# Two-layer retention and convolution backbone on one core: output and down projections by seven products, with the token sums made a stage earlier

## The chip, the cores and the metric

The kernel runs on one core of a Trainium2 chip. The metric is device time in microseconds (us) of one execution; for the kernel before, three runs gave 2707.88, 2707.94 and 2709.12, median 2707.94. Engines are called PE (TensorE, matrix products), DVE (VectorE), ACT (ScalarE), POOL (GpSimd) and SP (SyncE, which here only issues DMAs). PSUM, where PE accumulates, has eight banks of 128 x 512 fp32.

## What is computed

Two layers over 1024 latent tokens of width 1024, with a 256-token context that layer 0 reads. Layer 0 mixes tokens by retention (4 heads), layer 1 by a gated short convolution; each is followed by a SwiGLU FFN of hidden width 2816. Every sub-layer is modulated and gated by parameters made from `c`.

```python
def retention_output(o, g, w_o):
    o = o * lax.rsqrt(jnp.mean(o * o, axis=-1, keepdims=True) + EPS)
    o = o.transpose(0, 2, 1, 3).reshape(bsz, L, nh * dv).astype(g.dtype)
    return (jax.nn.silu(g) * o) @ w_o                      # (1024, 2048) @ (2048, 1024)

def conv_mixer(h, w_in, w_conv, w_out):
    b_gate, c_gate, xv = jnp.split(h @ w_in, 3, axis=-1)
    return (b_gate * short_conv(c_gate * xv, w_conv)) @ w_out   # (1024, 1024) @ (1024, 1024)

def swiglu(h, w1, w3, w2):
    return (jax.nn.silu(h @ w1) * (h @ w3)) @ w2           # (1024, 2816) @ (2816, 1024)

for i in range(DEPTH):
    ...
        hx = hx + g1 * yx
        fx = modulate(rms_norm(hx, norm_ffn[i]), sh2, sc2)
        hx = hx + g2 * swiglu(fx, ffn_w1[i], ffn_w3[i], ffn_w2[i])
    ...
return rms_norm(hx, final_norm)
```

## The kernel before

All data are fp32. Every operand of a product is split into two fp32r parts by `split`: ACT casts the high part (L131), DVE subtracts it from the operand for the low part (L132; sometimes POOL does). `mm3` (L136 to L138) then makes one product as three matmuls: high by low, low by high, high by high.

Activations lie transposed: a tile holds 128 features by a block of 512 tokens, and there are two token blocks (`tb` 0 and 1). A product makes one output tile of 128 features by 512 tokens in one PSUM bank, by accumulating over the tiles `kt` of the contraction, 128 features each.

The stages run one after another: context layer; projections v, q, k, g; retention scan, head by head; w_o; the up products of FFN0 (w1, w3); its down projection (w2); conv in; conv out; FFN1 up; FFN1 down with the final norm. The up products and the projections into the mixers are made by `winograd`: the operands are cut into 2 x 2 blocks (features by token blocks), seven products of sums of blocks stand for eight, and DVE (POOL for every second one) makes the sums of x (`x_sums`), DVE the sums of weights (L478 to L484). The first blocks of each up stage are plain, by `linear`, since the sums of x need both token blocks.

w_o, w2 and the conv output weights go through `out_proj` (L1125), with all eight plain products. Its contraction is cut into ranges of at most six tiles (`R_O`, `R_F`, `R_C`). In a range, each of eight output tiles by two token blocks is one product over the range, then one DVE instruction (L1167) multiplies the bank by the gate and adds it to the residual tile in H. In the last range the token blocks come one after the other: the first one's squares are summed (`sq_add`, L256 ACT and L257 DVE), the norm is made from them (`rstd_diag`: PE L262, the DVE steps L267 and L142 to L154, the diagonal tiles L280; `spread`: PE L288), and the next stage's operands are modulated (L293) while the other block's products run. In FFN1, the second token block goes in two halves of 256 tokens (`PARTS`), and `result_tile` and `result_end` turn and scale the output.

Tiles pass between stages by DRAM: `og_d` holds the gated heads, `u_d` the products of the up stages, `h_d` the residuals. DMAs to DRAM go out on ACT's queue, loads on SP's. The modulation parameters are dot products on DVE (`ada_next`, L202, 80 weight tiles of 512 KB), two instructions of 512 columns for each tile; they run in the projections v and g and in the ranges of w_o and w2 of FFN0.

What stands beside what is set by hand: `hooks` is a queue of small steps (loads, splits, sums), and after each product `unit_done` runs one or more of them; `until` runs steps until a condition holds. A scheduler then orders each engine's instructions.

The quoted lines give `mm3` and the evictions:

```python
def mm3(ps, w_hi, w_lo, x_hi, x_lo, first, last, group=True):
    nc.tensor.matmul(ps, w_hi, x_lo, start=first, stop=False, **kw)
    nc.tensor.matmul(ps, w_lo, x_hi, start=False, stop=False, **kw)
    nc.tensor.matmul(ps, w_hi, x_hi, start=False, stop=last, **kw)
```

## Time and profile before

| what | value |
|---|---|
| median of three runs | 2707.94 us |
| the profiled execution | 2709.07 us |
| its span, first to last instruction | 2707.3 us |
| mean granted PE clock | 0.996 |
| PE busy | 2660.1 us, 98% |
| DVE busy | 1759.5 us, 65% |
| ACT busy | 1094.4 us, 40% |
| POOL busy | 203.7 us, 8% |
| DMA | 366.94 MB, mean 136 GB/s |

The stages begin, by their first matmuls, at these times of the span: retention 597, w_o 829.6, FFN0 up 1014.7, FFN0 down 1446.7, conv in 1688.0, conv out 1929.1, FFN1 up 2018.1, FFN1 down 2450.0, end 2707.3. Matmuls are pipelined: one of 512 columns is shown 0.39 us long, while the next starts 0.23 us after it. A clock of 1.00 in a row of the trace is the full 2.4 GHz.

### The profile page before, as it was taken

The page shows a single profiled execution, that of the slowest core. Times are in us where ns is not written, and L with a number is a line of the kernel's source. Part 1 is how long each engine was busy: PE and PEld are TensorE (multiplying, and loading weights), DVE is VectorE, ACT ScalarE, POOL GpSimd, SP SyncE. Part 2 cuts the span into 40 slices and gives each one's busy share as a digit, 9 for nine tenths or more (in the row PEclk, how much of TensorE's full clock was granted, in tenths as well). Part 3 has the DMA queues.
Part 4 walks back from the last instruction along what each step waited for, and adds up shares of the span by engine and source line. Part 5 has one row for each costly group of instructions (what it writes and reads, how often), then busy time and mean ns, then how long its engine had stood idle before and what let it go on. Part 6 is the DMA issues. An engine that isn't in the chain of part 4 may idle for free.

```text
span 2707.3 us, 32651 instructions
## 1 busy us (share of the span) xinstructions
PE 2660.1 (98%) x11952; PEld 2182.1 (81%) x11952; DVE 1759.5 (65%) x3033; ACT 1094.4 (40%) x2006; POOL 203.7 (8%) x142
## 2 busy tenths in 40 slices
PE   8999999999999999999999999999999999999998
PEld 4788888877777887888888888788887888888887
DVE  4876777768887758555557655876767555556435
ACT  4642333447874225333334222533434333343212
POOL 1210221002220002000000000200002000000000
PEclk9999999999999999999999999999999999999999
DMA  9546235664668622222228522222522222236211
GB/s 332 187 162 219 81 106 194 237 221 131 194 201 284 203 85 102 83 77 86 82 78 286 172 86 98 74 87 70 171 101 97 82 86 78 90 102 202 82 47 63
DMA packets 167393, 366.94 MB, mean 136 GB/s; under 512 B 17600, under 2 KB 35136, under 8 KB 167232
## 3 DMA queue, kind: packets, MB, share of 16 engines
q1 hardware_dynamic: 109872, 283.78, 32.1%
q10 hardware_dynamic: 57360, 81.07, 8.3%
q8 instruction: 94, 1.54, 0.2%
q14 instruction: 67, 0.55, 0.1%
HBM read 281.94 MB, written 82.84 MB: 135 GB/s over the span
## 4 chain that ended last, share of the span: by engine, by line
PE 53%; DVE 5%; issue 3%; ACT 1%; POOL 0%; ACTq 0%; DVEq 0%; POOLq 0%
PE ps L136 18%; PE ps L137 18%; PE ps L138 18%; DVE u L132 3%; ACT u L131 0%; DVE tt L439 0%; DVE t L293 0%; POOL u L132 0%; DVE t L443 0%; PE ps L288 0%; DVE t L439 0%; PE ps L262 0%; DVE tt L1265 0%; DVE tt L293 0%; PE ps L1296 0%
## 5 line engine op out<-in xcount | busy, mean ns | idle before, releaser
L136 PE MATMUL ps<-u 128*128 128x512 f32 (+1 forms) x3640 | 1422.8, 391 | 18.2 <-DVE tt L522 9.0
L137 PE MATMUL ps<-u 128*128 128x512 f32 (+1 forms) x3640 | 1413.0, 388 | 0.4 <-DVE u L132 0.4
L138 PE MATMUL ps<-u 128*128 128x512 f32 (+1 forms) x3640 | 1411.7, 388 | 0.0
L136 PEld LDWEIGHTS ps<-u 128*128 128x128 f32 x3640 | 684.9, 188 | 166.7 <-DVE tt L522 9.4
L137 PEld LDWEIGHTS ps<-u 128*128 128x128 f32 x3640 | 685.3, 188 | 141.0 <-issue 2.2
L138 PEld LDWEIGHTS ps<-u 128*128 128x128 f32 x3640 | 685.1, 188 | 140.9
L131 ACT CAST u<-raw 128x512 fp32r<-128x512 f32 (+1 forms) x770 | 447.0, 603 | 758.8 <-PE ps L138 457.7
L132 DVE TENSOR_TENSOR u<-raw,u 128x512 fp32r<-128x512 f32 (+1 forms) x770 | 517.6, 690 | 268.4 <-ACT u L131 265.5
L1167 DVE SCALAR_TENSOR_TENSOR t<-ps,ada,t 128x512 f32<-128x512 f32 (+1 forms) x162 | 117.9, 728 | 147.1 <-PE ps L138 146.4
L519 ACT COPY tt<-ps 128x512 f32<-128x512 f32 x174 | 102.1, 587 | 254.2 <-PE ps L138 247.5
L132 DVE TENSOR_TENSOR u<-tt,u 128x512 fp32r<-128x512 f32 x200 | 138.6, 728 | 44.2 <-ACT u L131 43.8
L131 ACT CAST u<-tt 128x512 fp32r<-128x512 f32 x206 | 119.0, 620 | 74.6 <-DVE tt L439 24.2
L202 DVE SCALAR_TENSOR_TENSOR raw<-raw,c_row 128x512 f32<-128x512 f32 x160 | 104.8, 685 | 47.6 <-DMA raw<-in_ada_t 47.4
L532 DVE TENSOR_TENSOR tt<-tt,ps 128x512 f32<-128x512 f32 x58 | 39.8, 686 | 119.0 <-PE ps L138 119.0
L749 DVE SCALAR_TENSOR_TENSOR u<-ps,u 128x512 fp32r<-128x512 f32 x128 | 84.8, 684 | 27.4 <-ACT u L748 27.3
L132 POOL TENSOR_TENSOR u<-tt,u 128x512 fp32r<-128x512 f32 x6 | 7.8, 1298 | 1149.0 <-DMA raw<-in_w_ci 623.1
L748 ACT ACTIVATE u<-ps 128x512 fp32r<-128x512 f32 x128 | 73.8, 596 | 26.9 <-PE ps L138 24.8
L526 DVE TENSOR_TENSOR tt<-tt,ps 128x512 f32<-128x512 f32 x58 | 39.8, 687 | 65.3 <-ACT tt L519 65.3
L698 POOL TENSOR_TENSOR u<-t,u 128x512 fp32r<-128x512 f32 x40 | 55.4, 1390 | 307.2 <-DMA t<-v_d 139.6
L257 DVE TENSOR_TENSOR tt<-tt 128x512 f32<-128x512 f32 (+1 forms) x70 | 48.3, 690 | 29.0 <-ACT tt L256 28.6
L1167 DVE SCALAR_TENSOR_TENSOR tt<-ps,ada,tt 128x512 f32<-128x512 f32 (+1 forms) x54 | 39.3, 729 | 41.6 <-PE ps L138 41.1
L256 ACT ACTIVATE tt<-t 128x512 f32<-128x512 f32 (+1 forms) x54 | 31.5, 583 | 83.7 <-DVE t L1167 71.9
(138 smaller groups left out, 1686.3 us busy)
## 6 DMA issues: line engine op xcount, KB each, us to landing
raw<-in_w SPq DMA_DIRECT2D x88, 512.0 KB, 3.8
raw<-in_ada_t SPq DMA_DIRECT2D x80, 512.0 KB, 5.1
u_d<-tt ACTq DMA_DIRECT2D x104, 256.0 KB, 2.0
tt<-u_d SPq DMA_DIRECT2D x104, 256.0 KB, 4.6
raw<-in_w_v SPq DMA_DIRECT2D x36, 512.0 KB, 4.9
raw<-in_w SPq DMA_DIRECT2D x48, 384.0 KB, 4.5
raw<-in_w_ci SPq DMA_DIRECT2D x24, 512.0 KB, 3.8
v_d<-tt ACTq DMA_DIRECT2D x40, 256.0 KB, 3.7
```

The lines of the kernel that those rows point to most:

```text
L131: nc.scalar.copy(dst_hi, src)
L132: (eng or nc.vector).tensor_sub(dst_lo, src, dst_hi.bitcast(F32))
L136: nc.tensor.matmul(ps, w_hi, x_lo, start=first, stop=False, **kw)
L137: nc.tensor.matmul(ps, w_lo, x_hi, start=False, stop=False, **kw)
L138: nc.tensor.matmul(ps, w_hi, x_hi, start=False, stop=last, **kw)
L202: nc.vector.scalar_tensor_tensor(w[:, k], w[:, k], 1.0, c_row[:, k], op0=ALU.mult, op1=ALU.mult, accum_out=sums[:, e, ct : ct + 1],)
L257: eng.tensor_tensor(acc[:, :n], acc[:, :n], s[:, :n], op=ALU.add)
L519: nc.scalar.copy(m[p, n], ps)
L698: nc.gpsimd.tensor_sub(t[:, 1], v, t[:, 0].bitcast(F32))
L748: nc.scalar.activation(s[:, 0], st[d][m], AF.Copy, scale=f)
L749: nc.vector.scalar_tensor_tensor(s[:, 1], st[d][m], f, s[:, 0].bitcast(F32), op0=ALU.mult, op1=ALU.subtract,)
L1167: nc.vector.scalar_tensor_tensor(h, ps, gate[:, kt : kt + 1], h, op0=ALU.mult, op1=ALU.add)
```

## The change

`out_proj` with its ranges, `dram_steps`, `early_steps` and the halves of the last token block go. A new `down` makes w_o (`nh` = 8), both w2 (`nh` = 11) and the conv output projection (`nh` = 4) by seven products in the order 1, 5, 6, 3, 7, 2, 4. The contraction's tiles are the outer loop: one step is one contraction tile of one product for four output tiles, 12 matmuls into a set of four banks. Set A takes products 1, 6, 7 and 4, which go on accumulating in the same banks; set B takes 5 and 3, and then 2 anew. After each product the four banks are evicted into H, whatever has accumulated by then (L1202 of the changed kernel, whose line numbers the pieces of order below have).

The x operand of a step is loaded from DRAM as a ready sum. The stage before makes those sums: `take` collects four tiles, and two steps make four subtractions on DVE, spilled to `x_d` by ACT's queue. For w_o, `o_steps` loads the finished heads again and makes the sums; the first 16 in the third head, the others after the last one. Sums of weights are made in `operands` on DVE, three steps ahead.

38 of the 80 parameter tiles move from w_o and w2 into FFN0's up products (`also`). The two FFNs take token block 1 first.

```diff
+    D_ORDER = (1, 5, 6, 3, 7, 2, 4)
+    D_OUT = {1: (0, 0), 5: (1, 1), 6: (0, 1), 3: (0, 1), 7: (1, 1), 2: (0, 0), 4: (1, 0)}
+    D_AHEAD = 3
+    D_LOADS = 3
...
+        def operands(m):
+            x_loads(m + 1, True)
+            x_loads(m + 1 + D_LOADS)
...
+            n, i = seq[m]
+            xs[m] = in_parts(xl.pop(m))
+            wa, wc = wr[i][:, :512], wr[i][:, 512:]
+            if n != 1:
+                wb, wd = wr[nh + i][:, :512], wr[nh + i][:, 512:]
+            if n == 5:
+                nc.vector.tensor_add(wc, wc, wd)
+            elif n == 6:
+                nc.vector.tensor_sub(wc, wc, wa)
+            if n in (3, 7):
+                t = ttile()
+                nc.vector.tensor_sub(t, wb if n == 3 else wd, wc)
+            else:
+                t = wa if n == 1 else {5: wc, 6: wc, 2: wb, 4: wd}[n]
+            ws[m] = in_parts(t)
...
+        def run():
+            banks = {}
+            for m, (n, i) in enumerate(seq):
+                which = "A" if n in (1, 6, 7, 4) else "B"
...
+                    if n == 5:
+                        until(lambda: src(2, nh - 1) is not None)
+                    if n in (1, 5, 2):
+                        banks[which] = [bank() for _ in range(4)]
...
+                    if n == 4:
+                        hooks.extend(norm_steps(order[1]))
...
+                until(lambda: m in ws)
+                operands(m + D_AHEAD)
+                w, x = ws.pop(m), xs.pop(m)
+                for c in range(4):
+                    k = slice(c * P, (c + 1) * P)
+                    mm3(
+                        banks[which][c], w[:, 0, k], w[:, 1, k], x[:, 0], x[:, 1],
+                        n in (1, 5, 2) and i == 0, i == nh - 1, False,
+                    )
+                if i == nh - 1:
+                    for c in range(4):
+                        kt = 4 * j + c
+                        h = H[kt, tb]
+                        nc.vector.scalar_tensor_tensor(
+                            h, banks[which][c], gate[:, kt : kt + 1], h, op0=ALU.mult, op1=ALU.add
+                        )
+                        if n in (3, 7, 2, 4):
+                            complete(kt, tb)
+                unit_done(2 if n == 4 or n == 1 or nh == 4 else 1)
...
+                def one():
+                    nc.vector.tensor_sub(x12, x12, x11)
+                    put(5, pr, x12)
+                    nc.vector.tensor_sub(x22, x22, x12)
+                    put(6, pr, x22)
+
+                def two():
+                    nc.vector.tensor_sub(x11, x22, x11)
+                    put(7, pr, x11)
+                    nc.vector.tensor_sub(x21, x21, x22)
+                    put(4, pr, x21)
...
+            hooks.extend(lambda h=h, c=c: finish(h, c) for c in range(NCH))
+            hooks.append(lambda h=h: o_ready.add(h))
+            if h % 2:
+                loads, sums = zip(*(o_steps(h // 2 * 4 + i) for i in range(4)))
+                hooks.append(loads[0])
+                for i in range(1, 4):
+                    hooks.extend(grouped([loads[i], sums[i - 1]], 2))
+                hooks.append(sums[3])
```

First piece, DVE in FFN0's down projection. L126 makes low halves (L132 before), L1126 the weight sums of products 3 and 7, L1202 evicts (L1167 before), L258 adds squares (L257 before). Before, around the middle of that stage:

```order
L1167 SCALAR_TENSOR_TENSOR t_12452<-ps,ada_5_91,t_12452 128x512
L132 TENSOR_TENSOR u<-raw,u 128x256
L132 TENSOR_TENSOR u<-raw,u 128x512
L132 TENSOR_TENSOR u<-tt,u 128x512 x4
L1167 SCALAR_TENSOR_TENSOR t_12454<-ps,ada_5_91,t_12454 128x512
L132 TENSOR_TENSOR u<-tt,u 128x512 x3
L202 SCALAR_TENSOR_TENSOR raw,ada<-raw,c_row 128x512 x3
```

Now, where product 3 ends and product 7 begins:

```order
L1126 TENSOR_TENSOR tt<-raw 128x512 x2
L126 TENSOR_TENSOR u<-tt,u 128x512 x6
L1202 SCALAR_TENSOR_TENSOR t_13063<-ps,ada_5_91,t_13063 128x512
L1202 SCALAR_TENSOR_TENSOR t_13065<-ps,ada_5_91,t_13065 128x512
L1202 SCALAR_TENSOR_TENSOR t_13067<-ps,ada_5_91,t_13067 128x512
L1202 SCALAR_TENSOR_TENSOR t_13069<-ps,ada_5_91,t_13069 128x512
L258 TENSOR_TENSOR tt<-tt 128x512 x2
L1126 TENSOR_TENSOR tt<-raw 128x512
L258 TENSOR_TENSOR tt<-tt 128x512
L1126 TENSOR_TENSOR tt<-raw 128x512
L126 TENSOR_TENSOR u<-tt,u 128x512 x4
```

One eviction at a time between operands has become four together with their squares, and the operands of the three steps that follow stand ahead of them.

Second piece, the end of the conv output projection, on DVE. L267 or L268 starts the norm, L142 to L154 or L136 to L148 are its small steps, L280 or L281 the diagonals, L293 or L294 the modulation. Before:

```order
L154 SCALAR_TENSOR_TENSOR rs_y<-rs_u,rs_y 128x4
L1167 SCALAR_TENSOR_TENSOR t_15754<-ps,ada_2_94,t_15754 128x512
L150 TENSOR_TENSOR rs_u<-rs_y 128x4
L151 SCALAR_TENSOR_TENSOR rs_u<-rs_u,rs_v 128x4
L154 SCALAR_TENSOR_TENSOR rs_y<-rs_u,rs_y 128x4
L280 TENSOR_SCALAR tt<-ident,rs_y 128x128 x4
L257 TENSOR_TENSOR tt<-tt 128x512
```

Now; the four evictions are product 4's:

```order
L1202 SCALAR_TENSOR_TENSOR t_16715<-ps,ada_2_94,t_16715 128x512
L144 TENSOR_TENSOR rs_u<-rs_y 128x4
L1202 SCALAR_TENSOR_TENSOR t_16717<-ps,ada_2_94,t_16717 128x512
L145 SCALAR_TENSOR_TENSOR rs_u<-rs_u,rs_v 128x4
L1202 SCALAR_TENSOR_TENSOR t_16719<-ps,ada_2_94,t_16719 128x512
L148 SCALAR_TENSOR_TENSOR rs_y<-rs_u,rs_y 128x4
L1202 SCALAR_TENSOR_TENSOR t_16721<-ps,ada_2_94,t_16721 128x512
L144 TENSOR_TENSOR rs_u<-rs_y 128x4
L145 SCALAR_TENSOR_TENSOR rs_u<-rs_u,rs_v 128x4
L148 SCALAR_TENSOR_TENSOR rs_y<-rs_u,rs_y 128x4
L281 TENSOR_SCALAR tt<-ident,rs_y 128x128 x4
```

Then PE at the same place; ps_16197 is the last bank of product 4, ps_16896 the spread norm and ps_16998 the first plain product of FFN1:

```order
L130 MATMUL ps_16197<-u_16838,u_16841 128x512
L131 MATMUL ps_16197<-u_16838,u_16841 128x512
L132 MATMUL ps_16197<-u_16838,u_16841 128x512
L289 MATMUL ps_16896<-tt_16879,ones_86 128x512
L130 MATMUL ps_16998<-u_16898,u_16751 128x512
L131 MATMUL ps_16998<-u_16898,u_16751 128x512
```

The last evictions stand among the norm's steps, and no matmul of the projection is left when PE comes to the spread.

Third piece, the start of w_o on DVE. Before, L794 gates the last head's pieces:

```order
L794 SCALAR_TENSOR_TENSOR tt<-t_7205,ys_538,tt 128x512
L132 TENSOR_TENSOR u<-raw,u 128x512
L794 SCALAR_TENSOR_TENSOR tt<-t_7121,ys_538,tt 128x512
L794 SCALAR_TENSOR_TENSOR tt<-t_7036,ys_538,tt 128x512
L132 TENSOR_TENSOR u<-raw,u 128x512
```

Now, after the end of product 1 (L1411 to L1417 are the sums of heads 2 and 3, L1121 and L1123 the weight sums of products 5 and 6, or 5 alone):

```order
L1202 SCALAR_TENSOR_TENSOR tt<-ps,ada_2_88,tt 128x512 x3
L1411 TENSOR_TENSOR raw<-raw 128x512
L126 TENSOR_TENSOR u<-tt,u 128x512
L126 TENSOR_TENSOR u<-raw,u 128x512
L1413 TENSOR_TENSOR raw<-raw 128x512
L1202 SCALAR_TENSOR_TENSOR tt<-ps,ada_2_88,tt 128x512
L1415 TENSOR_TENSOR raw<-raw 128x512
L1417 TENSOR_TENSOR raw<-raw 128x512
L1411 TENSOR_TENSOR raw<-raw 128x512
L1121 TENSOR_TENSOR raw<-raw 128x512
L1413 TENSOR_TENSOR raw<-raw 128x512
```

Sums of heads stand between evictions and operands of w_o.

## Rows read from the trace of the kernel before

**Rows 1.** Page, busy time (share of the span), instructions of PE and DVE.
```profile
PE 2660.1 (98%) x11952; PEld 2182.1 (81%) x11952; DVE 1759.5 (65%) x3033; ACT 1094.4 (40%) x2006; POOL 203.7 (8%) x142
```
**Rows 2.** Busy time by stretch of the span: FFN0 up, FFN0 down, FFN1 down.
```profile
core 0: us, PE busy (x) PEld busy (x) DVE busy (x) ACT busy (x) POOL busy (x), PEclk, DMA share, GB/s
...
1075.00:1435.00 360.00, 360.00 (x1586) 297.93 (x1585) 201.22 (x307) 135.76 (x235) 0.00 (x0) 1.00 0.26 86
1435.00:1680.00 245.00, 245.00 (x1083) 202.29 (x1082) 140.81 (x281) 61.87 (x115) 0.00 (x0) 1.00 0.47 157
...
2440.00:2660.00 220.00, 220.00 (x971) 181.85 (x970) 96.64 (x153) 51.60 (x98) 0.00 (x0) 1.00 0.30 101
```
**Rows 3.** PE's waits: line, releaser, us in total, times, longest us.
```profile
PE ps L136 <- DVE tt L522: 9.0, 4, 2.7
...
PE ps L799 <- DVE tt L794: 8.1, 8, 1.4
```
**Rows 4.** Timeline, conv in: start us, us, instruction; DVE twice, then ACT.
```profile
1741.20 0.68 DVE L484 TENSOR_TENSOR raw<-raw 128x512 f32<-128x512 f32 x1
1741.80 0.68 DVE L1366 TENSOR_TENSOR tt<-tt,ps 128x512 f32<-128x512 f32 x1
...
1740.59 0.62 ACT L131 CAST u<-raw 128x512 fp32r<-128x512 f32 x1 [2.52 <-DVE raw L480]
```
**Rows 5.** Page, costliest groups: busy, mean ns, idle before; DVE's low halves.
```profile
L132 DVE TENSOR_TENSOR u<-raw,u 128x512 fp32r<-128x512 f32 (+1 forms) x770 | 517.6, 690 | 268.4 <-ACT u L131 265.5
```
**Rows 6.** Timeline of DVE and POOL at the end of conv out.
```profile
2034.41 2.06 DVE L293 SCALAR_TENSOR_TENSOR t<-t,ada,ps 128x512 f32<-128x512 f32 x3
...
2038.62 1.78 DVE L132 TENSOR_TENSOR u<-t,u 128x512 fp32r<-128x512 f32 x1
...
2038.55 1.29 POOL L132 TENSOR_TENSOR u<-t,u 128x512 fp32r<-128x512 f32 x1
```
**Rows 7.** DVE by line and form in FFN0 down, 1460 to 1680.
```profile
L1167 DVE SCALAR_TENSOR_TENSOR t<-ps,ada,t 128x512 f32<-128x512 f32 x44 | 32.9, 749 | 39.1 <-PE ps L138 38.9
L202 DVE SCALAR_TENSOR_TENSOR raw<-raw,c_row 128x512 f32<-128x512 f32 x39 | 25.5, 686 | 13.1 <-DMA raw<-in_ada_t 13.1
```
**Rows 8.** Busy time, one 58 us stretch of retention.
```profile
661.00:719.00 58.00, 56.30 (x264) 46.05 (x263) 50.38 (x86) 47.51 (x100) 14.11 (x10) 1.00 0.63 192
```
**Rows 9.** DVE by line and form in retention, 661 to 777.
```profile
L794 DVE SCALAR_TENSOR_TENSOR tt<-t,ys,tt 128x512 f32<-128x512 f32 x16 | 18.2, 1135 | 0.1
...
L132 DVE TENSOR_TENSOR u<-tt,u 128x512 fp32r<-128x512 f32 x12 | 9.9, 862 | 0.0
```
**Rows 10.** POOL by line and form in the same stretch.
```profile
L698 POOL TENSOR_TENSOR u<-t,u 128x512 fp32r<-128x512 f32 x20 | 28.3, 1417 | 87.1 <-ACT u L697 62.8 <-DMA tt<-k_d 22.1 <-PE ps L799 2.3
```
**Rows 11.** DMA issues: count, KB each, median us from issue to landing.
```profile
og_d<-tt ACTq DMA_DIRECT2D x32, 256.0 KB, 4.3
tt<-og_d SPq DMA_DIRECT2D x32, 256.0 KB, 5.0
```
**Rows 12.** Busy time, end of retention and start of w_o.
```profile
815.00:830.00 15.00, 12.47 (x54) 9.67 (x53) 13.95 (x25) 12.85 (x29) 0.00 (x0) 1.00 0.79 241
835.00:860.00 25.00, 20.88 (x103) 16.22 (x103) 12.59 (x33) 8.19 (x16) 0.00 (x0) 1.00 0.81 263
```
**Rows 13.** Timeline of DVE at the start of w_o.
```profile
852.90 1.54 DVE L794 SCALAR_TENSOR_TENSOR tt<-t,ys,tt 128x512 f32<-128x512 f32 x2 [4.81 <-DMA tt<-g_d]
```
**Rows 14.** Busy time, end of conv out and start of FFN1 up.
```profile
2018.00:2075.00 57.00, 54.49 (x239) 43.66 (x238) 52.65 (x81) 31.15 (x55) 18.28 (x12) 1.00 0.33 110
```
**Rows 15.** Busy time, the last block's halves and what follows.
```profile
2667.00:2697.00 30.00, 29.27 (x237) 28.06 (x235) 24.27 (x70) 13.79 (x33) 0.00 (x0) 1.00 0.27 101
2697.00:2707.30 10.30, 1.53 (x10) 1.06 (x9) 4.08 (x16) 2.08 (x4) 0.00 (x0) 0.72 0.32 117
```
**Rows 16.** Busy time right behind a 3 us wait of PE.
```profile
1073.00:1077.00 4.00, 4.00 (x12) 3.14 (x11) 1.39 (x2) 1.28 (x3) 0.00 (x0) 0.57 0.16 33
```

## The prediction before the run

> **What bounds the kernel now.** I read the shares of busy time first: TensorE (PE) is busy for 2660.1 of 2707.3 us, VectorE (DVE) for 1759.5 [rows 1]. Next the table by stage, where the reader is to see that PE is busy without a gap in the long stretches, in the down projection of FFN0 (1435 to 1680) as in the up products before it, while DVE is busy for little over half of them [rows 2]. Last PE's waits: the longest groups amount to 9.0 and 8.1 us [rows 3]. So the bound is the count of matmuls, and what can spoil a smaller count is DVE (all combinations, evictions and the low halves of the operand splits), where it works for a stage's end or start. The profiled execution took 2709.07 us, 1.1 above the median of the three runs (2707.94); the sum is made against 2709.07.
>
> **Removed matmuls.** Eight multiplications become seven. The 512-wide ones go from 10728 to 10416, and 192 of 256 columns go, 96 whole ones' worth. Per projection: w_o 768 to 672, each w2 1056 to 924, conv out 384 to 336; together 3264 to 2856, 408 fewer. Three long stretches hold 1586 + 1083 + 971 = 3640 matmuls in 825 us, so 0.2266 us each [rows 2]; 408 x 0.2266 = **-92.5**. A step of the new loop is 12 matmuls, 2.72 us.
>
> **DVE inside the new loop.** Back to back, a DVE combination costs 0.60 from start to start [rows 4] (0.69 by itself [rows 5]), an eviction from PSUM 0.66 (2.06 for three, where one by itself has 0.75) [rows 6, 7]. A step needs two low halves, and in products 5, 6, 3 and 7 one combination more: 1.8 us of 2.72. Each product ends in four evictions (2.6), in four products with four squares sums too (2.4). The first order piece shows what DVE has done before product 3's evictions: the operands are issued three steps ahead, so 8.2 us of matmuls lie against some 6.3 of evictions, sums and the next operands. PE has the other set of banks to go on with. I take +1 for each of the two w2 stages, +1 for w_o, whose product 4 lasts 8 steps, bounds 0 and 6 for the three; together **+3**. The evictions themselves become fewer (204 to 112), and 136 combinations of weights are added, all inside the cover just named.
>
> **Sums made by the preceding stage.** FFN0's up products get 44 subtractions (27 us) and the 38 moved ada steps (two DVE instructions of about 0.7 each [rows 7], with their accumulator reads 1.45, so 55 us): 201 + 27 + 55 = 283 of some 385 us, all beside matmuls. Cost 0, and if that cover went, 82 us of DVE work would stand against 100 idle ones. Conv and FFN1 up have only the subtractions. The spills to x_d go out by ACT's queue, 214 in place of the 104 to u_d; ACT is busy for 136 of 360 us there [rows 2]; 0.
>
> **Retention, the third head.** The sums of heads 0 and 1 (16 subtractions, 8 loads, 16 spills) fall where DVE has no room: a 58 us stretch of this stage has DVE at 50.4 [rows 8], so 7.6 free per head. Two-input combinations are dearer there, 862 ns, and L794 takes 1135 [rows 9], while GpSimd runs its own at 1417 [rows 10]. 16 x 0.862 = 13.8; less 7.6 is **+6**. Bounds +2 (the work spreads over both of the heads left) and +15 (each takes as long as GpSimd's own, 16 x 1.417 = 22.7, less 7.6).
>
> **Start of w_o.** The sums for heads 2 and 3 need the last head finished: store 4.3, load 5.0 [rows 11], then four combinations, then spill. The third order piece shows them between the operands of product 5, ahead of evictions on DVE's queue. At that place the DMA engines are already 0.79 and 0.81 busy at 241 and 263 GB/s [rows 12], and DVE waited 4.81 us for a g_d load [rows 13]. The change puts some 28 transfers of 256 KB (7.3 MB, at 263 GB/s 28 us) into the stretch before the last head's first gate load. Products 1 and 5 last 16 x 2.72 = 44 us, which covers most of it. I take **+6**, near the 4.81 that a late load cost there; bounds 0 (the products cover all) and 20 (the 28 us less the 8 that the waits leave today).
>
> **End of conv out.** Here nh is 4 and product 4 has only 10.9 us of matmuls. The second order piece shows its four evictions among the small steps of the other token block's rsqrt chain, and the PE order puts the spread of that block's norm right behind product 4's last matmul, where w_o and both FFNs still have 68 or more matmuls to go. So PE waits for 4 x 0.66 + six small steps of 0.2 + the diagonal 0.9 = 4.8. Then the first plain product (24 matmuls, 5.4 us) needs eight modulated tiles: 8 x 0.66 + 4 squares sums and 5 low halves at 0.6, and three locks with GpSimd of about 1.1 (a low half took 1.78 beside GpSimd's 1.29 [rows 6]) = 14, so 8.6 more. Together +13.4. The stretch is DVE's already today, 52.65 of 57 us with 2.5 of PE idle [rows 14]. **+13.4**, bounds 5 (the scheduler's order runs looser than it reads) and 20.
>
> **The tail.** The last token block's two halves go. From 2667 the kernel took 30.0 + 10.3 = 40.3 us [rows 15] for 96 whole matmuls' worth (21.8), so 18.5 beside them. Now: 2.6 for the first block's output transposes, 1.6 for two waits as today, and after the last matmul 8 evictions and squares (5.3), today's 10.3, and two more output tiles (1.4): 21.1. **+2.6**, bounds 0 and 6.
>
> **Clock.** After a PE wait of about 3 us (the longest today is 2.7 [rows 3]) the granted clock of the next 4 us was 0.57 [rows 16], so mostly the lower of the two levels (1.2 GHz, where 2.4 shows as 1.00): 12 matmuls took 4.0 us in place of 2.72, and a little more of it lies outside that window; some 1.5 us each time. Two such new waits, conv out and w_o: **+3**.
>
> **Sum.** -92.5 + 3 + 6 + 6 + 13.4 + 2.6 + 3 = -58.5, so 2709.07 - 58.5 = 2650.6; the median lies about 1 lower: **2650**.
>
> **Rivals.**
> *Everything hides.* DVE is at half load in the long stretches [rows 2], and operands stand steps ahead, so the waits named could be 0 or 1 us each: -92.5 + 2.6 gives 2619, 2618 as a median. Against it speak the two places where DVE is full [rows 8, 14].
> *DVE is late at each stage's end and start.* All upper bounds of the stages' edges: retention 15, w_o 20, conv out 20, w2 and w_o inside 6, tail 6, clock 6: 73, so 2689. The crowded queues there speak for it [rows 9, 12, 14]; that w_o and both FFNs have ample matmuls left behind their norm speaks against. Part of it only, 2675 to 2690.
> *GpSimd and DVE shut each other out in the third head.* L794 takes 1135 ns where a two-input instruction elsewhere takes 690 [rows 5, 9], as though it waited for part of a GpSimd one. If each of a head's ten GpSimd instructions cost the 16 new subtractions 1.1 us (1.417 and the handing over, less part of a DVE one), they would take 16 x 0.69 + 10 x 1.1 = 22 in place of 13.8, the term would be +14 and the median 2658. The long means speak for waits [rows 9], but the low halves' 862 says that most instructions meet none. The Trainium skill, "SBUF — State Buffer", "Who interferes with whom", says that a DVE instruction with two SBUF inputs contends with a GpSimd instruction that reads SBUF, and that the loser is blocked in full. By that rule the new subtractions are all exposed; the longer means [rows 9] agree with it as far as they go.
> *Slower: the operands are made in series.* A combining step is cast, low half, combination, then cast and low half of it, where each waits for the one before: 0.62 [rows 4] + 0.69 + 0.69 + 0.62 + 0.69 = 3.31 against 2.72 of matmuls. If steps don't overlap, the 136 steps of products 5, 6, 3 and 7 (4 x 34) lose 0.59 each, 80 us, and with the other costs (34) the kernel is at 2731. It decides from 3.15 us a step on, where the loss eats the 58. The order speaks against: combinations of later steps stand ahead of the low halves of earlier ones, and two engines share the chain.
> *The change does not do what it says.* Were the matmuls not fewer, the time would be 2709 and more; the built order counts 408 fewer, so this is nearly out.
>
> **How the numbers follow.** Forecast case 0.48 (2630 to 2672, where a term or two lies at a bound), the third head's lock 0.10, everything hides 0.16, DVE late at the edges 0.20, series 0.04, no change 0.02. What a measurement of this kernel can tell is about 0.2%, 5.4 us. The range 2616 to 2690 takes in the first four but for their tails, and leaves out the last two (0.06). Faster 0.94, same 0.02, slower 0.04.
>
> **What would show it.** In the profile after: 2856 matmuls in the four projections, at 0.2266 us each in the long windows; PE without gaps inside the w2 stages, one gap of about 5 us and a first plain product of about 14 behind conv out; DVE's busy time in the third head close to its span; the first wait in w_o at product 5. I am wrong in the term if conv out's end shows no gap, wrong in the bound if PE falls below 0.98 busy inside a w2 stage, and wrong in the count if a step takes other than 2.72.

## The result, and the profile after

| | us |
|---|---|
| before, median of four runs (2707.88 to 2713.73) | 2708.53 |
| the change, median of four runs (2674.46 to 2683.47) | 2679.97 |
| ratio, 95% interval | 0.9889, 0.9867 to 0.9910 |
| the change's profiled execution, its span | 2674.46, 2672.7 |

The change is faster by 1.1%, 28.6 us by the medians; the forecast was 58. The profiled execution lies at the low end of its own runs, 34.6 us below before's profiled one. That difference can be laid out by stage, from the first matmul of each stage to the first of the next ("of it matmuls" is what the smaller count saves at 0.2266 us each, "rest" what is lost beside it):

| stage | before | change | difference | of it matmuls | rest |
|---|---|---|---|---|---|
| up to retention | 597.1 | 598.2 | +1.0 | 0 | +1.0 |
| retention | 232.5 | 242.5 | +10.0 | 0 | +10.0 |
| w_o | 185.1 | 181.3 | -3.8 | -21.8 | +18.0 |
| FFN0 up, seven products | 386.0 | 392.5 | +6.5 | 0 | +6.5 |
| FFN0 down | 241.2 | 212.2 | -29.0 | -29.9 | +0.9 |
| conv out, then FFN1's plain products | 135.0 | 139.6 | +4.6 | -10.9 | +15.5 |
| FFN1 up, seven products | 385.9 | 392.2 | +6.3 | 0 | +6.3 |
| FFN1 down, to the end | 257.3 | 229.7 | -27.6 | -29.9 | +2.3 |
| FFN0 plain, conv in | 287.2 | 284.5 | -2.7 | 0 | -2.7 |

The matmuls came out as counted. The rest, +58, ate most of the gain. The page's first line after the change, against [rows 1]: PE is busy for 74 us less, DVE for 195 us more.

```profile
PE 2586.1 (97%) x11448; PEld 2109.5 (79%) x11448; DVE 1954.4 (73%) x3354; ACT 1189.2 (44%) x2162; POOL 202.5 (8%) x142
```

PE's waits after the change (line, releaser, us in total, times, longest), against [rows 3]. The first row is the same wait for the first combining step of the up stages that was 9.0 in total. Of the next, L724's stands in the third head, L126's 10.1 half in w_o (4.1) and half in conv out (5.0); the long ones of L131 and of ACT (4.3 and 4.1) stand in w_o. L289 is the spread norm at conv out's end.

```profile
PE ps L130 <- DVE tt L496: 17.6, 4, 8.1
PE ps L130 <- DVE u L724: 11.9, 8, 4.2
PE ps L130 <- DVE u L126: 10.1, 6, 3.1
...
PE ps L131 <- DVE u L126: 5.1, 3, 4.3
PE ps L130 <- ACT u L125: 4.3, 2, 4.1
PE ps L289 <- DVE tt L281: 3.8, 2, 2.4
```

Busy time by stretch after the change; the columns are those of [rows 2], and the rows answer to [rows 2, 8, 12, 14, 16]: FFN0 down, the third head (two stretches, the trouble begins at 755), the start of w_o, conv out's end, and the 4 us behind an 8 us wait.

```profile
core 0: us, PE busy (x) PEld busy (x) DVE busy (x) ACT busy (x) POOL busy (x), PEclk, DMA share, GB/s
...
1459.00:1672.00 213.00, 212.89 (x939) 175.22 (x938) 162.52 (x271) 104.17 (x186) 4.40 (x3) 1.00 0.49 158
...
714.00:772.00 58.00, 52.01 (x236) 42.00 (x235) 46.62 (x82) 41.70 (x85) 13.23 (x10) 0.97 0.77 241
772.00:800.00 28.00, 21.42 (x87) 16.17 (x86) 25.45 (x49) 15.82 (x34) 5.91 (x4) 0.94 0.84 286
841.00:900.00 59.00, 42.00 (x176) 31.57 (x175) 38.67 (x71) 14.70 (x28) 0.00 (x0) 0.88 1.00 343
1989.00:2046.00 57.00, 50.74 (x200) 40.10 (x199) 49.15 (x80) 31.27 (x54) 19.15 (x13) 0.88 0.22 72
2067.50:2071.50 4.00, 3.99 (x9) 3.14 (x10) 1.95 (x3) 1.75 (x3) 0.00 (x0) 0.50 0.26 96
```

The long loop is as good as hoped: PE has 212.89 of 213 us in FFN0 down, with DVE at 162.5. At w_o's start the DMA engines are busy without a break (1.00, 343 GB/s) while PE has 42 of 59 us. Neither there nor at conv out's end is DVE full. ACT at w_o's start stands behind spills of the sums, which its queue holds ahead of this cast (start us, us, instruction, idle before and releaser):

```profile
883.29 0.62 ACT L125 CAST u<-tt 128x512 fp32r<-128x512 f32 x1 [13.48 <-DMA x_d<-raw]
```

What holds the first combining step of FFN1 up is seen on DVE's timeline of the change (start us, us, instruction, idle before and releaser):

```profile
2058.88 0.67 DVE L1296 TENSOR_TENSOR tt<-tt,ps 128x512 f32<-128x512 f32 x1
2059.48 1.28 DVE L126 TENSOR_TENSOR u<-raw,u 128x512 fp32r<-128x512 f32 x2
2060.68 0.68 DVE L458 TENSOR_TENSOR raw<-raw 128x512 f32<-128x512 f32 x1
2061.28 0.68 DVE L452 TENSOR_TENSOR raw<-raw 128x512 f32<-128x512 f32 x1
2064.84 0.69 DVE L1241 TENSOR_TENSOR tt<-tt 128x512 f32<-128x512 f32 x1 [2.88 <-DMA x_d<-tt]
2065.57 0.69 DVE L1245 TENSOR_TENSOR tt<-tt 128x512 f32<-128x512 f32 x1
2066.18 0.68 DVE L1247 TENSOR_TENSOR tt<-tt 128x512 f32<-128x512 f32 x1
2066.78 0.68 DVE L496 TENSOR_TENSOR tt<-tt,ps 128x512 f32<-128x512 f32 x1
```

L1296 makes the last tile of the first pair, which is then spilled. L1241 subtracts into that same tile, so it waits for the spill: 2.88 us of idle DVE, at the head of its queue. L496, for which PE waits, stands behind it and behind two more new subtractions. The combining step's result was due about 2059.5 (PE's last matmul ahead of it began at 2059.04).

At conv out's end, DVE of the change shows this:

```profile
1986.85 0.16 DVE L148 SCALAR_TENSOR_TENSOR rs_y<-rs_u,rs_y 128x4 f32<-128x4 f32 x1
1990.74 0.75 DVE L1202 SCALAR_TENSOR_TENSOR t<-ps,ada,t 128x512 f32<-128x512 f32 x1 [3.73 <-PE ps L132]
...
1992.94 0.75 DVE L1202 SCALAR_TENSOR_TENSOR t<-ps,ada,t 128x512 f32<-128x512 f32 x1
...
1993.99 0.16 DVE L148 SCALAR_TENSOR_TENSOR rs_y<-rs_u,rs_y 128x4 f32<-128x4 f32 x1
1994.19 0.87 DVE L281 TENSOR_SCALAR tt<-ident,rs_y 128x128 f32<-128x128 f32 x4
```

The norm's chain stands still from 1987.0 to 1990.7, since the evictions of product 4 come next in the order and wait for PE; then PE waits for the rest of the chain. The second order piece showed just that. But conv out lost time at its start as well: from 1911 to 1935 PE came 4.2 us short of back-to-back matmuls, where before it lost none. ACT there waits for a tile that goes from the conv stage to x_d and back:

```profile
1919.97 0.62 ACT L125 CAST u<-tt 128x512 fp32r<-128x512 f32 x1 [10.09 <-DMA tt<-x_d]
```

So of conv out's +15.5 some 4 lie at its start and 11 at its end.

The FFNs' up stages lost 6.5 and 6.3 us, but not in the same places. FFN1 lost all of it in its first 17 us; FFN0 lost 3.6 there and some 2.5 a hundred microseconds later, where the moved parameter steps and their loads run. FFN0's stretch, then FFN1's at the same place:

```profile
1160.00:1190.00 30.00, 28.54 (x125) 22.98 (x124) 27.16 (x67) 10.39 (x19) 0.00 (x0) 1.00 0.85 282
```

```profile
2143.00:2173.00 30.00, 30.00 (x134) 24.86 (x133) 19.43 (x30) 11.43 (x20) 0.00 (x0) 1.00 0.34 115
```

### The profile page after: what moved, and what is told of

Its sections match the earlier page's. It is cut to its first block, busy times and chain, and to the rows that moved or that the text cites. A ratio compares the mean times of both kernels' runs of the same rounds, so it can differ in the third digit from the quotient of the medians.

```text
span 2672.7 us, 32986 instructions
## 1 busy us (share of the span) xinstructions
PE 2586.1 (97%) x11448; PEld 2109.5 (79%) x11448; DVE 1954.4 (73%) x3354; ACT 1189.2 (44%) x2162; POOL 202.5 (8%) x142
## 4 chain that ended last, share of the span: by engine, by line
PE 77%; DVE 10%; DMA 6%; issue 4%; ACT 2%; POOL 0%; SPq 0%; ACTq 0%; DVEq 0%; POOLq 0%
PE ps L130 25%; PE ps L131 25%; PE ps L132 25%; DVE u L126 3%; DVE t L203 1%; PE ps L230 1%; DMA raw<-og_d 1%; ACT u L125 1%; DMA tt<-x_d 1%; DMA og_d<-tt 1%; DMA raw<-in_w 1%; PE ps L954 1%; DVE tt L412 1%; DMA raw<-in_w_o 0%; DVE u L724 0%
## 5 line engine op out<-in xcount | busy, mean ns | idle before, releaser
L130 PE MATMUL ps<-u 128*128 128x512 f32 x3472 | 1365.9, 394 | 48.0 <-DVE tt L496 17.6
L131 PE MATMUL ps<-u 128*128 128x512 f32 x3472 | 1360.7, 392 | 5.2 <-DVE u L126 5.1
L132 PE MATMUL ps<-u 128*128 128x512 f32 x3472 | 1357.2, 391 | 0.0
L130 PEld LDWEIGHTS ps<-u 128*128 128x128 f32 x3472 | 655.3, 189 | 197.3 <-DVE tt L496 18.5
L131 PEld LDWEIGHTS ps<-u 128*128 128x128 f32 x3472 | 656.0, 189 | 144.3 <-DVE u L126 8.4
L132 PEld LDWEIGHTS ps<-u 128*128 128x128 f32 x3472 | 655.8, 189 | 137.8 <-issue 0.7
L125 ACT CAST u<-raw 128x512 fp32r<-128x512 f32 x772 | 466.6, 619 | 562.4 <-PE ps L132 265.8
L126 DVE TENSOR_TENSOR u<-raw,u 128x512 fp32r<-128x512 f32 x772 | 541.1, 713 | 170.7 <-ACT u L125 168.9
L125 ACT CAST u<-tt 128x512 fp32r<-128x512 f32 x394 | 232.3, 619 | 252.6 <-issue 60.1
L126 DVE TENSOR_TENSOR u<-tt,u 128x512 fp32r<-128x512 f32 x391 | 278.2, 737 | 81.0 <-ACT u L125 79.0
L126 POOL TENSOR_TENSOR u<-t,u 128x512 fp32r<-128x512 f32 x15 | 21.2, 1414 | 1093.9 <-ACT u L125 1093.1
L724 DVE SCALAR_TENSOR_TENSOR u<-ps,u 128x512 fp32r<-128x512 f32 x128 | 84.5, 685 | 25.3 <-ACT u L723 25.3
L1202 DVE SCALAR_TENSOR_TENSOR t<-ps,ada,t 128x512 f32<-128x512 f32 x80 | 56.0, 746 | 52.8 <-PE ps L132 52.8
L673 POOL TENSOR_TENSOR u<-t,u 128x512 fp32r<-128x512 f32 x40 | 55.1, 1382 | 318.2 <-ACT u L672 312.6
L203 DVE SCALAR_TENSOR_TENSOR raw<-raw,c_row 128x512 f32<-128x512 f32 x84 | 55.1, 687 | 21.0 <-DMA raw<-in_ada_t 20.9
L130 PE MATMUL ps<-u,kh 128*128 128x512 f32 x144 | 56.8, 395 | 1.0 <-issue 1.0
L132 PE MATMUL ps<-u,kh 128*128 128x512 f32 x144 | 56.6, 393 | 0.0
L131 PE MATMUL ps<-u,kh 128*128 128x512 f32 x144 | 56.6, 393 | 0.0
```

What stands on the lines that cost most here:

```text
L125: nc.scalar.copy(dst_hi, src)
L126: (eng or nc.vector).tensor_sub(dst_lo, src, dst_hi.bitcast(F32))
L203: nc.vector.scalar_tensor_tensor(w[e], w[e], 1.0, c_row[:, k], op0=ALU.mult, op1=ALU.mult, accum_out=sums[:, e, ct : ct + 1],)
L673: nc.gpsimd.tensor_sub(t[:, 1], v, t[:, 0].bitcast(F32))
L724: nc.vector.scalar_tensor_tensor(s[:, 1], st[d][m], f, s[:, 0].bitcast(F32), op0=ALU.mult, op1=ALU.subtract,)
L1202: nc.vector.scalar_tensor_tensor(h, banks[which][c], gate[:, kt : kt + 1], h, op0=ALU.mult, op1=ALU.add)
```

## The experiments

Each is an edit of the changed kernel. Stage times are of the profiled executions, read as in the table above; where a kernel left these two stages alone, retention took 241.8 to 244.3 us and w_o 181.3 to 184.4, so differences of 3 us there are scatter. Ratios are to before.

**A fresh tile for the first difference (e1_fresh_tile).**

```diff
-                    nc.vector.tensor_sub(x22, x22, x12)
-                    put(6, pr, x22)
+                    y[0] = ttile() if pr == 0 else x22
+                    nc.vector.tensor_sub(y[0], x22, x12)
+                    put(6, pr, y[0])
```

> Edit: for the first pair of tiles of each up stage, the difference x22 - x12 goes into a fresh tile, so that it no longer has to wait until the spill of x22 has been read. Same work, same order otherwise. Theory (the subtraction waits for its own spill and stands ahead of the first combination of the seven products): PE's pause before the first combining product of FFN0 and FFN1 up falls from 6.8 and 8.5 us to about 3.1, which conv in shows, and each of the two stages gets shorter by about 6, the kernel by 11 to 13. Rival (DVE is simply late there with its backlog of sums and low halves): the pauses stay above 5.5 and the kernel gains less than 4.

Median 2673.4, ratio 0.9870 (0.9851 to 0.9889); its runs (2669.7 to 2679.4) overlap the change's, so the gain is read from the stages. FFN1 up fell from 392.2 to 388.6 us and its pause (from the start of PE's last matmul before the combining step to the next) from 8.5 to 5.4; FFN0 up stayed (392.9), its pause fell only from 6.8 to 6.0. Where a kernel left these places alone, the pauses were 7.0 to 8.5 in FFN1 and 6.5 to 8.4 in FFN0. DVE in FFN1:

```profile
2058.73 0.67 DVE L1299 TENSOR_TENSOR tt<-tt,ps 128x512 f32<-128x512 f32 x1
...
2061.13 0.68 DVE L1244 TENSOR_TENSOR tt<-tt 128x512 f32<-128x512 f32 x1
...
2063.54 0.67 DVE L496 TENSOR_TENSOR tt<-tt,ps 128x512 f32<-128x512 f32 x1
```

The wait for the spill is gone, which shows that part. L496 still comes 4.2 us late, behind seven instructions in place of three before the change, among them three of the new subtractions. In FFN0, two instructions of the moved parameter steps stood in the queue as well. So the theory holds for up to 3 us of FFN1's pause. For the rest the rows show a longer queue ahead of L496; that it alone makes the pause is not shown by this run.

**The same subtractions issued later (e5_first_pair_late).**

```diff
-                hooks.extend([one, two])
+                hooks.extend([nothing, nothing, one, two] if pr == 0 else [one, two])
...
-            elif n % 3 == 0:
+            elif n % 3 == 0 and n >= 6:
```

> Edit: in the FFNs, the four subtractions on the first pair of tiles come two products later, and the first moved parameter step comes at the seventh product instead of the fourth. No fresh tile. Theory (what stands between the last plain product's result and the first combining step on DVE's queue makes PE wait, part of it the wait of a subtraction for its own spill, part the subtractions and parameter steps themselves): PE's pause falls from 6.8 and 8.5 us to 3.1 in both FFNs, FFN0's and FFN1's up stages each lose 6 us, the kernel 12. Rival (the pause comes from low halves and weight sums that were already there): the pause stays above 5 in both and the kernel gains less than 4.

Median 2683.0, ratio 0.9904 (0.9889 to 0.9919): nothing gained, pauses 6.8 and 8.3. The two rows of DVE in FFN1 show why: the scheduler put the subtraction into the same place ahead of L496 although the step queue has it later.

```profile
2071.80 0.69 DVE L1241 TENSOR_TENSOR tt<-tt 128x512 f32<-128x512 f32 x1 [2.65 <-DMA x_d<-tt]
...
2073.74 0.68 DVE L496 TENSOR_TENSOR tt<-tt,ps 128x512 f32<-128x512 f32 x1
```

The experiment did not change what it meant to, so it decides nothing between the theories.

**The subtractions on GpSimd (e10_pool_sums).**

```diff
+                eng = nc.gpsimd if pr == 0 else nc.vector
...
-                    nc.vector.tensor_sub(x22, x22, x12)
+                    eng.tensor_sub(x22, x22, x12)
...
+            eng = nc.gpsimd if nh == 4 else nc.vector
...
-                nc.vector.tensor_add(wc, wc, wd)
+                eng.tensor_add(wc, wc, wd)
```

> Edit: GpSimd instead of DVE makes the four subtractions of each up stage's first pair and conv out's 16 combinations of weights; the moved parameter steps begin at the tenth product. Theory (DVE's queue in order is what holds PE at these places): PE's pause before the first combining step falls from 6.8 and 8.5 us to 3 to 4.3 in the FFNs, each up stage gets shorter by 4 to 6; conv out with the plain stage of FFN1 falls from 139.6 us to 131 to 136; the kernel gains 11 to 18. Rival (a two-input DVE instruction and a GpSimd one keep each other waiting, or the scheduler puts other DVE work into the place): the pauses stay above 5, the conv part above 138.

Median 2682.2, ratio 0.9901 (0.9886 to 0.9916); FFN0 up got longer, 398.6 us; conv out with the plain stage 138.5. The wait only changed its queue. GpSimd first, then ACT, in FFN1:

```profile
2073.68 1.28 POOL L1244 TENSOR_TENSOR tt<-tt 128x512 f32<-128x512 f32 x1 [7.37 <-DMA x_d<-tt]
...
2076.30 1.29 POOL L1250 TENSOR_TENSOR tt<-tt 128x512 f32<-128x512 f32 x1
```

```profile
2075.00 2.94 ACTq L1229 DMA_DIRECT2D x_d<-tt  x3
2077.99 0.63 ACT L1294 ACTIVATE tt<-tt 128x512 f32<-128x512 f32 x1 [5.06 <-POOL tt L1250]
```

DVE's L496 now comes earlier, and of FFN1's 8.1 us of waiting for it 1.3 are left (PE, from 2056 to 2110):

```profile
PE ps L130 <- DVE tt L496: 1.3, 1, 1.3
```

So there the subtractions on DVE's queue were what PE waited for. But ACT issues the spills, in order, and stood 5.06 us behind GpSimd's last subtraction; the casts that the next products need stand behind that, PE waited 3.9 us for ACT in the same stretch, and FFN1 up took 391 us, hardly less than the change's 392.2.

**The third head without subtractions (e3_no_subs), with spills from SP (e8_spill_sp), without any of it (e4_no_pair0).**

```diff
         def sums():
+            if i < 4:
+                put(5, t[0, 1])
...
+                return
```

> Edit: in the third head, the 16 subtractions on the tiles of heads 0 and 1 are left out and the loaded tiles are spilled as they are; the output is another one. Loads and spills stay. Theory A (DVE is the bound of the third head, by the subtractions' work and by their waits for the loads at the head of its queue): retention falls from 242.5 us to 231 to 234, the kernel by 8 to 11. Theory B (the 32 more transfers crowd the queues and delay the scan's own loads): retention stays above 239.

```diff
-            nc.scalar.dma_start(x_d[n - 1][i], src)
+            (nc.sync if i < 4 else nc.scalar).dma_start(x_d[n - 1][i], src)
```

> Edit: the 16 spills of the sums of heads 0 and 1 in the third head are issued by SP instead of ACT; loads, subtractions and bytes are the same. Theory A (the spills hold ACT's queue for 1.0 to 1.4 us each, ahead of ACT's part of the scan, so that DVE and then PE wait for ACT): retention falls from 242 to 245 us to 231 to 236, the kernel by 7 to 11. Theory B (the DMA engines' load delays the scan's own tiles): retention stays above 240, whoever issues.

```diff
+        if i < 4:
+            return o_tile(i, 1)
...
-            if h % 2:
+            if h == 3:
```

> Edit: nothing is loaded, subtracted or spilled for heads 0 and 1 in the third head; products 5, 6, 7 and 4 of w_o read the heads' own tiles in place of these sums, so the output is another one. Both theories of the third head give retention at 229 to 233 us here, 10 to 13 less than with the sums; the difference to the run without the subtractions is the transfers' share. If retention stays above 238, the loss is in the fourth head, by the early loads for w_o.

Retention took 244.0, 244.5 and 228.8 us (w_o then took 187.2 in the last, so that it gave back part); the medians are 2680.4, 2681.9 and 2664.7 (ratios 0.9892, 0.9904 and 0.9837, the last 0.9822 to 0.9852). The same 36 us of the third head, in the change, without subtractions, from SP, and without any of it:

```profile
758.00:794.00 36.00, 25.25 (x91) 18.47 (x89) 28.84 (x56) 18.12 (x40) 7.03 (x5) 0.91 0.88 298
```

```profile
758.00:794.00 36.00, 25.01 (x94) 18.75 (x92) 21.80 (x36) 18.51 (x42) 6.90 (x5) 0.86 0.93 310
```

```profile
758.00:794.00 36.00, 24.28 (x93) 17.61 (x91) 32.78 (x59) 19.74 (x43) 8.67 (x6) 0.95 0.91 307
```

```profile
758.00:794.00 36.00, 34.30 (x160) 27.84 (x159) 32.63 (x58) 30.89 (x64) 12.53 (x9) 1.00 0.55 169
```

Without the subtractions DVE falls to 21.8 us and PE stays at 25; ACT then stands behind its spills:

```profile
776.68 5.66 ACTq L1407 DMA_DIRECT2D x_d<-raw  x4
782.44 0.63 ACT L753 ACTIVATE tt<-t 128x512 f32<-128x512 f32 x1 [7.81 <-DMA x_d<-raw]
```

With the spills on SP, ACT is free of them, but DVE has 32.8 of 36 us and PE still 24. As the rows read, neither one alone is the bound: take away DVE's work and the queue that spills holds PE, take away the spills from ACT and DVE holds it, each to within 2 us of the same length. Both gone, with the loads too, PE has 34.3. By their retention times both runs came out as the other theory on record said, that transfers delay the scan's own tiles. The waits speak against it as the main cause: from 745 to 800 ACT waited 1.5 us for such a tile (k_d) without the subtractions, DVE 1.3 (g_d) and GpSimd 2.8 (v_d) with the spills on SP. But the run without any of it had less traffic too (0.55 for 0.88 in these 36 us), and subtractions and spills without the loads were not tried, so the two limits are read from waits and not shown by an edit.

The subtractions themselves were not dear. Two of their four lines in the change, from 714 to 800; the other two have means of 683 and 681 ns and no idle time:

```profile
L1413 DVE TENSOR_TENSOR raw<-raw 128x512 f32<-128x512 f32 x4 | 3.7, 930 | 2.4 <-DMA raw<-og_d 2.4
L1411 DVE TENSOR_TENSOR raw<-raw 128x512 f32<-128x512 f32 x4 | 2.7, 687 | 2.2 <-DMA raw<-og_d 2.2
```

All 16 took 11.8 us, and DVE stood 4.6 us for their loads. One of them took 1.65 us, beside a GpSimd instruction.

**The start of w_o: other heads (e2_early_heads) and another order (e6_o_order).**

```diff
-                    nc.sync.dma_start(t[k, tb], og_of(i // 4 * 8 + k * 4 + i % 4, tb))
+                    nc.sync.dma_start(t[k, tb], og_of(k * 4 + i % 4, tb))
```

> Edit: the sums for heads 2 and 3 are made from the tiles of heads 0 and 1, which have long been in DRAM; the output is another one. Same number of loads, subtractions and spills, at the same places of the queue of steps. Theory A (the last head's chain finish, store, load, subtract, spill is too long): PE's pauses between 874 and 898 go, the w_o stage falls from 181 us to about 168, the kernel by 10 to 14. Theory B (the DMA engines are full from 841 to 900, so that bytes set the time): the bytes are the same, the pauses only move, and the stage stays above 177.

```diff
+        grouped(pair_steps(w_plain, a["w1"][0, 0], KT), 2), prods=(1, 2, 5, 6, 3, 7, 4),
...
+                if n == 1 and early2:
+                    w_load(nh + i, 0)
+                if n == (2 if early2 else 1):
+                    w_load(i, 1)
+                    w_load(nh + i, 1)
```

> Edit: w_o alone goes through its products in the order 1, 2, 5, 6, 3, 7, 4, so that the sums of heads 2 and 3 and half of the weights are needed 8 steps (21.8 us) later; the bytes of the whole stage are the same. Theory A (a burst of transfers at the start of w_o, more than the DMA engines carry in that time): PE's pauses between 870 and 900 fall from 14 us to under 4, the stage from 181 to 184 us to 168 to 172, the kernel by 10 to 14. Rival (the order of instructions on DVE and ACT holds PE, whatever the bytes, with product 2 and product 5 sharing a set of banks): the pauses move and stay above 9, the stage above 177.

With other heads' tiles the w_o stage took 184.1 us (median 2681.1, ratio 0.9897), no better, although no sum's load needed the last head's tiles. PE's share at the start is the same, with the same full DMA engines:

```profile
845.00:905.00 60.00, 42.91 (x177) 31.91 (x175) 38.23 (x71) 14.94 (x29) 0.00 (x0) 0.89 1.00 348
```

That takes away the long chain of the last head as the cause and fits the bytes. The other order did not give the proof I hoped for: 188.2 us, median 2687.7, ratio 0.9923 (0.9908 to 0.9938), slower than the change. The spills of the sums stayed where they were in ACT's queue, now ahead of the casts of product 2; ACT's waits (us in total, times, longest) from 840 to 910:

```profile
ACT u L125 <- DMA x_d<-raw: 19.1, 2, 17.9
```

The change itself has 13.48 us of that wait. So at w_o's start two things stand together, full DMA engines and spills in order ahead of casts, and these runs do not part them; spills from another queue were not tried there.

**Conv out in another order (e7_co_order).** Beside the line shown, `down` gets what the order needs, as in the run before.

```diff
+        prods=(1, 5, 6, 3, 7, 4, 2),
```

> Edit: conv out alone goes through its products in the order 1, 5, 6, 3, 7, 4, 2, so that two products of 10.9 us each, instead of one, stand behind the end of the first normalized token block. Product 4 then follows 7 in the same banks. Theory (the norm's chain on DVE behind product 7's evictions is longer than one product of four steps): PE's pauses at the end of conv out and in the first plain product fall from about 8 us to 2, conv out and the plain stage of FFN1 together from 139.6 to 128 to 131 us, the kernel by 8 to 11. Rival (DVE is full over the whole stage, so the norm is late anyway, or product 4 waits for the evictions of product 7): the sum stays above 135.

Median 2680.9, ratio 0.9898 (0.9883 to 0.9912); conv out with the plain stage 139.0 us against 139.6. FFN1's plain products got cheaper (47.3 for 51.5), but PE waited 3.9 us for product 7's evictions in the shared banks, and the scheduler again put evictions, now product 4's, among the norm's steps (L1209 evicts here):

```profile
1986.41 0.15 DVE L144 TENSOR_TENSOR rs_u<-rs_y 128x4 f32<-128x4 f32 x1
1986.48 0.74 DVE L1209 SCALAR_TENSOR_TENSOR t<-ps,ada,t 128x512 f32<-128x512 f32 x1
...
1990.30 0.87 DVE L281 TENSOR_SCALAR tt<-ident,rs_y 128x128 f32<-128x128 f32 x4
```

More matmuls behind the norm were no help while its chain stood interleaved with evictions, and the start of conv out still lost some 3 us; what the order alone is worth stays open.

**w_o undone (e9_plain_wo), with GpSimd's sums (e11_both), and w_o and conv out undone (e12_final).** The edit of the first puts back `out_proj` and the retention loop of before for w_o:

```diff
-    o_run()
+    out_proj(
+        og_of, R_O, a["w_o"], mods[0, 2], modulator(fx, mods[0, 4], mods[0, 3]),
+        lambda kt, tb: a["xT"][kt, tb], pre=(xs_first, first),
+        then=grouped(pair_steps(w_plain, a["w1"][0, 0], KT), 2),
+    )
```

> Edit: w_o alone is undone, with the plain eight products in ranges, its weights and the retention loop as in the kernel before; the three other projections keep seven products and their sums, the parameter steps stay where the change put them. 96 more matmuls (21.8 us) than with the change. Theory A (the transfers and subtractions for w_o's sums cost about 13 us in the third head and 18 to 21 at w_o's start, more than the matmuls they save): retention returns to 229 to 233 us, w_o takes 183 to 187, and the kernel gains 8 to 15 on the change. Rival (what is lost there comes from elsewhere, such as the run's own scatter): the kernel gets slower by 10 to 22.

Median 2666.6, ratio 0.9837 (0.9822 to 0.9851), 13.4 us below the change with 96 matmuls more. Retention took 229.2 us and w_o 184.3; the start of w_o has PE at 55.7 of 59 us:

```profile
826.00:885.00 59.00, 55.68 (x257) 45.05 (x256) 37.16 (x72) 23.69 (x49) 0.00 (x0) 1.00 0.81 273
```

So seven products at w_o were a loss: 21.8 us saved, more than 30 given back in two stages.

> Edit: both of the two before, w_o undone and the sums on GpSimd. If the parts are as separate in time as the stages say, the gains on the change add up to within 3 us, and the kernel is at 2650 to 2662, faster than either kernel. If they are not, it stays within 5 us of the better of the two.

Median 2673.4, ratio 0.9866 (0.9850 to 0.9883). GpSimd's sums cost w_o undone 7 us more, some 5 of it in FFN0 up with 399.5 us; there was no gain of theirs to add, and the run fits neither of the two cases expected.

The last kernel also puts back the plain products for conv out, and takes the fresh tile; the moved parameter steps begin at the 21st product:

```diff
-            take(pr, j, tb, y)
+            nc.scalar.dma_start(u_d[pr * 2 + j][tb], y)
...
-    c_run()
+    out_proj(
+        u_of, R_C, a["w_co"], mods[1, 2], modulator(fx, mods[1, 4], mods[1, 3]), h_of,
+        early=early, then=grouped(pair_steps(w_plain, a["w1"][1, 0], KT), 2),
+    )
```

> Edit: w_o and conv out with the plain eight products and their own stores and loads as in the kernel before (conv's tiles re-paired by the order of the weights' rows), both w2 with the change's seven products, the first pair's difference in a fresh tile in the FFNs. 144 more matmuls (32.7 us) than with the change. Theory (seven products pay only where the contraction is long and the stage before has room; at w_o and conv out they give back more than they save): against the run with w_o undone alone (2666.6 us), conv out with the plain stage of FFN1 falls from 139.5 us to 134 to 136, FFN1's up stage by 2 to 4 by the fresh tile; median 2655 to 2662, the fastest of all. Rival (conv out's seven products pay after all): conv out with the plain stage stays at 139 or more, and the median at 2664 or more.

Median 2659.8 of five runs (2656.5 to 2664.4), ratio 0.9820 (0.9806 to 0.9833): the fastest, 20 us below the change with 144 matmuls more. Conv out with the plain stage took 135.0 us, as before the change, 4.6 less than with seven products; FFN0 up took 391.6 us, and FFN1 up 389.4, only 0.9 less than with w_o undone alone, where 2 to 4 were expected: that run's pause in FFN1 was 7.0 already, and the fresh tile made it 5.4. FFN0's pause stayed at 6.0, with a parameter step still ahead of the combining step on DVE, though its turn came later. The waits show what is left of the change's cost, the first combining steps:

```profile
PE ps L134 <- DVE tt L555: 13.4, 3, 5.6
```

## Why the prediction was right or wrong

The direction and the range (2616 to 2690) held; the size did not, 28.6 us for 58, and the time lies outside the forecast case's own 2630 to 2672. By its steps:

- **Removed matmuls**, -92.5: right; the two w2 stages bring -29.0 and -27.6. (The evictions counted beside it, 204, are 216 in before's page; no term goes by them.)
- **DVE inside the new loop**, +3 for three stages: right. FFN0 down lost 0.9, and PE was busy for 212.89 of 213 us. The rival of operands made in series is out.
- **Sums made by the preceding stage**, cost 0: this step failed, +12.8 in the two FFNs. I set the work against the whole stage's idle time; what counted is the first pair, whose sums come just ahead of the first combining step on DVE's queue. A subtraction into a tile that is being spilled waits for the spill, and the queue behind it waits too. The trace of before has that pause, 2.7 us, and I named it only as a clock effect. That FFN0 up and FFN1 up lost nearly the same, 6.5 and 6.3, is chance: FFN0 lost less at its start, and some 2.5 more where DVE, with the moved parameter steps, is at 27 of 30 us; that the steps cost these is not shown by an edit.
- **Retention**, +6 with bounds 2 and 15: +10.0 against before, 13 to 15 against the runs without the sums (the stage's first 17 us were 3 faster with the change). The size was near the upper bound, and the working was short of a mechanism: DVE's time alone does not explain it, since without the 16 subtractions the stage was no shorter, and DVE was not full (28.8 of 36 us), though the prediction named DVE close to its span as a sign. Left out were the waits at the head of the queues, DVE's for the loads and ACT's behind the spills. The rival of GpSimd and DVE gave +14, nearly the number, but not by its cause: it priced the 16 subtractions at 22 us, and they took 11.8. The Trainium skill's rule in "SBUF — State Buffer", "Who interferes with whom", is not refuted by that: one subtraction, beside a GpSimd instruction, took 1.65 us in place of 0.68. The loss here does not need it.
- **Start of w_o**, +6 with bounds 0 and 20, and 1.5 for the clock: +18.0. The transfers were named and counted, but "products 1 and 5 cover most of it" was wrong: the 59 us at 343 GB/s hold 20 MB, and PE lost 17 of them. What I took for one late load was a stretch in which the DMA engines had no gap, with ACT 13.48 us behind the spills of the sums; which of the two set the 17 us stays open. The Trainium skill, "DMA: Bandwidth & Descriptors", "Specifications", lists about 358 GB/s as a core's limit to HBM, half of what the memory stack gives two cores. The 343 and 348 measured here at a share of 1.00 lie just below it; since this kernel runs on one core, they do not show that it is the limit.
- **End of conv out**, +13.4 and 1.5 for the clock: +15.5 for the stage, but the size is luck in part. The end, as forecast in place, lost some 11 (the first plain product took 12.4 us where 14 were forecast); 4.2 lie at the stage's start, for which there was no term. At the end the order of DVE's queue, with an idle of 3.73 us, did more than a full DVE (49 of 57 us).
- **The tail** with FFN1 down's inside, +3.6: +2.3.
- **Clock**, two new waits: there were more, at the third head, at w_o, at the FFNs' starts and at conv out (0.94, 0.88, 0.50 and 0.88 in the rows above); the span's mean granted clock fell from 0.996 to 0.987, while the profiled execution with w_o and conv out undone is at 0.996 again.

In all +58 of rest where +34 was forecast: +13 from the FFNs' starts, +9 from w_o, +4 from retention, less some 2.5 elsewhere. Another 6 us lie between the profiled executions and the medians; the change's runs scatter by 9 us. So the range held because it took in a rival: the time falls where a late DVE at the edges had it (2675 to 2690). The places were that rival's, the cause only in part, since the traces show full DMA engines and waits at the head of queues more than DVE's work.

## What to carry to other kernels

Price work that is moved into a busy stage by the place where it lands in each queue, not by that stage's idle total: the first of it came just ahead of the instruction that PE waited for. Before you write a difference into the tile it was taken from, ask whether that tile is on its way to DRAM. Seven products paid where the contraction was long (11 tiles of pairs; 29.0 and 27.6 us of 29.9 kept, less the 6 that each up stage before lost). They lost at w_o, where the stage before had little DVE and DMA time to spare, and at conv out, with 4 tiles of pairs; undoing these two showed that they lost, not which of the waits there weighs most.

## What the runs showed that I had not expected

A stage can have limits so close together that taking one away changes nothing: retention was 244 us without the subtractions, 244 with the spills on another queue, 229 without both and without the loads. A store issued by a computing engine's queue held that engine until its source was ready: ACT stood 13.48 us behind spills at w_o's start, 7.81 behind four in the third head without subtractions, and 5.06 behind GpSimd's slower result. And the order in which steps are emitted did not set the order of DVE's queue: e5_first_pair_late moved a step by two products and found it where it had been.
